# Three heads instead of four biased on GpSimd in tiles 42 to 53 of a log-sum-exp kernel, and constant matmuls from tile 54 on

## The chip, the cores and the metric

The kernel runs on one core of a Trainium2 chip. A core has five engines that run side by side, each with its own queue of instructions in order: TensorE (PE; its weight loads are shown as PEld), VectorE (DVE), ScalarE (ACT), GpSimd (POOL) and SyncE (SP), which issues the loads and stores here. They work on SBUF; PE writes to PSUM, which VectorE and ScalarE can read. The metric is the device time of one execution in microseconds. Before the change three runs took 325.95, 326.36 and 326.98 us, so the median is 326.36 us.

## The reference

The input x has 8 batches of 2048 rows of 2048 columns in fp32 (134 MB), the columns being 8 heads of 256. A bias of 256 values per head is added, and for each row and head the logarithm of the sum of exponentials is taken. Each result is written twice in a row.

```python
x_heads = x.reshape(B, S, H, Dh).transpose(0, 2, 1, 3)
x_heads = x_heads + bias[None, :, None, :]
x_tiled = np.repeat(x_heads, 2, axis=2)
mx = x_tiled.max(axis=-1, keepdims=True)
lse = mx.squeeze(-1) + np.log(np.exp(x_tiled - mx).sum(axis=-1))
```

The output is 8 x 8 x 4096 in fp32. The kernel does not subtract the maximum; it keeps track of the smallest and largest sum and has a second, safe computation behind a branch at its end (`judge`, `all_again`) that is not taken with this data.

## The kernel before, in words

**Tiles.** The rows are cut into 64 tiles (t = 0 to 63) of 2 x 128 rows: 128 partitions, two rows (k = 0, 1) a partition, 2048 columns each, 2 MB a tile. Eight tiles have room in SBUF (`xbs`, seen as `xts`; the profile calls them xb). Up to tile 41 two tiles are loaded by one 4 MB transfer (L174), from tile 42 on each tile has its own, and from tile 57 on each row of a tile (L186); the last tile comes in pieces of columns (`LAST_COLS`). A load into a buffer waits for the last uses of the tile eight before (`last_uses`), and stands in SP's queue.

**The work on a tile.** For each head exp(x + bias) has to be summed over 256 columns. There are several ways to do it, and a dictionary per stage says how many heads go which way:

- Heads 0 to `pe`-1: PE puts the bias into PSUM by a matmul on ones (`put_bias`), adds x by a matmul with the identity, and ScalarE takes the exponential out of PSUM. For the first `acc` heads ScalarE sums as it goes (L373, L393, each followed by an accumulator read); the others go back to the tile in one exponential over two heads (L380).
- Heads from `g0` on: GpSimd adds the bias in place (`g_add`, L412), then ScalarE takes the exponential in place (L418), and VectorE sums with a reduction (L437).
- Heads between `pe` and `g0`: no bias is added. ScalarE takes the exponential of x, and the result is multiplied by exp(bias) (the factors, in `w_ps`, `one_ps` or `w_sb`).

**Stages.** `BULK` (tiles 0 to 53) has pe=3, acc=1, g0=4: heads 0 to 2 by PE, head 3 by a factor, heads 4 to 7 biased by GpSimd. The exponential of heads 3 to 7 is one ScalarE instruction of 2 x 1280 elements; VectorE then multiplies head 3 of both rows by its factor (L430, 512 elements) and sums heads 1 to 7 of both rows in one reduction (L437, 3584 elements). `MIXED` (54 to 56) has pe=1 and g0=4: heads 1 to 3 of each row are weighed and summed by one fused VectorE instruction a head and row (`weigh`, L453, 256 elements, with its accumulator read), and heads 4 to 7 are reduced by L437 (2048 elements). From tile 57 on GpSimd biases nothing; a row at a time, one to three heads go by PE and the rest by factors, weighed on VectorE or, for the last `fold` heads, multiplied and halved on GpSimd (L469, L477) and closed by a small VectorE reduction (L483).

**Order.** The order of instructions on each queue is the order of the program (`manual_schedule`). In the loop's round for tile t come: PE's additions of x; for tiles that aren't bulk, PE's bias of the next unit; GpSimd's addition for t; then what was put off from tile t-1 (`flush(for_pool)`, which runs `later` and with it ScalarE's large exponential of t-1, VectorE's work on it, and SP's reload); and then ScalarE's exponentials of the PE heads of t. From tile 57 on the PE heads of a row are taken by ScalarE only after the exponential of the next row. In round 54 PE also spreads the factors of heads 1 and 2 into `one_ps` (`first_factors`, L235), and ScalarE takes their exponential (L268).

**Constant matmuls.** `keep_warm` (L351 to L355) issues three matmuls of the identity with itself, whose result nobody reads, into the PSUM tile `tp`. It is called once for each row of tiles 57 to 63, after the bias of the next unit. An fp32 matmul is two instructions in the trace, so there are 84.

**The end.** When all sums of the last batch are there, PE transposes them (L606), ScalarE takes the logarithm (L612), SP stores them (L613), and VectorE and PE work out the verdict (L525 to L550).

Of the kernel before, what the change touches and what calls it, by code (L numbers as in the profile page):

```python
# [13 lines left out]
ALU = mybir.AluOpType  # L14
# [7 lines left out]
NBUF = 8  # L22

NEARLY = 5

NWARM = 3

# [1 line left out]

BULK = dict(pe=3, acc=1, g0=4, late=True, fold=0)
MIXED = dict(pe=1, acc=1, g0=4, late=False, fold=0)
PROMPT_F1 = dict(pe=2, acc=2, g0=8, late=False, fold=1)
PROMPT_F2 = dict(pe=2, acc=2, g0=8, late=False, fold=2)
# [9 lines left out]

STAGES = [
    (0, (BULK,)),
    (54, (MIXED,)),  # L50
    (57, (PROMPT_F1, PROMPT_F1)),
    (62, (SINGLE_F1, SINGLE_F1)),
# [10 lines left out]
def kernel(  # L63
# [6 lines left out]
    nc = tc.nc  # L70
    P = nc.NUM_PARTITIONS
    B, S, D = x.shape
    H, Dh = bias.shape
# [2 lines left out]
    NB = S // (P * KB)  # L76
    TB = KB // K
    T = B * NBLK
    T_PROMPT = STAGES[1][0]
    T_FACTORS = T // 2  # L80
    CPE = BULK["pe"] * Dh
    MM = 512
# [67 lines left out]
    def on_x(t, ins, after):  # L150
        buf = users[t // TB % len(xbs)]
        for t_u, u in buf:
            same = u.ins.engine == ins.ins.engine
            if u not in after and (not same or t_u % NBUF == t % NBUF and t_u < t):
                tc.declare_no_dep(
                    ins.ins,
                    u.ins,
                    reason="another tile, or waited for by those it waits for",
                )
        buf.append((t, ins))  # L160
        return ins
# [187 lines left out]
        return heads  # L349

    def keep_warm():  # L351
        for _ in range(NWARM):
            nc.tensor.matmul(  # L353
                tp[:, 0], lhsT=ident, rhs=ident, start=True, stop=True
            )  # L355

    def late_heads(m, t, got, sums):


        mms = []  # L360
        for h, p in enumerate(got[:-1]):
            mm = nc.tensor.matmul(  # L362
                p,
                lhsT=ident,
                rhs=xts[t % NBUF][:, :, h * Dh : (h + 1) * Dh],
                start=False,
                stop=True,
            )
            mms.append(on_x(t, mm, [loads[t, 0, 0]]))

        def pe_part():
            for k in range(K):
                act = nc.scalar.activation(  # L373
                    out=xts[t % NBUF][:, k, 0:Dh],
                    in_=got[0][:, k * Dh : (k + 1) * Dh],
                    func=ACT.Exp,
                    accum_out=sums[:, k, 0:1],
                )
                last_uses[t].append(on_x(t, act, [mms[0]]))
            act = nc.scalar.activation(  # L380
                out=xts[t % NBUF][:, :, Dh : m["pe"] * Dh].rearrange(
                    "p k (h j) -> p h k j", j=Dh
                ),
                in_=got[-1].rearrange("p (h k j) -> p h k j", k=K, j=Dh),
                func=ACT.Exp,
            )
            on_x(t, act, [mms[-1]])

        return pe_part

# [26 lines left out]
    def exp_inplace(t, v, after):  # L417
        return on_x(t, nc.scalar.activation(out=v, in_=v, func=ACT.Exp), [after])  # L418

    def later(m, t, k0, k1, sums, add):  # L420

        h0 = m["pe"] if m["late"] else m["g0"]
        v = xts[t % NBUF][:, k0:k1, h0 * Dh : D]
        done = exp_inplace(t, v, add)
        if m["late"]:
            n = (m["g0"] - h0) * Dh
            f = v[:, :, 0:n]
            h0 = m["acc"]
            v = xts[t % NBUF][:, k0:k1, h0 * Dh : D]
            mul = nc.vector.tensor_tensor(  # L430
                out=f,
                in0=f,
                in1=each_row(w_ps, m["pe"] * Dh - W0, n, k1 - k0),
                op=ALU.mult,
            )
            done = on_x(t, mul, [done])
        red = nc.vector.tensor_reduce(  # L437
            out=sums[:, k0:k1, h0:H],
            in_=v.rearrange("p k (h j) -> p k h j", j=Dh),
            op=ALU.add,  # L440
            axis=mybir.AxisListType.X,
        )
        last_uses[t].append(on_x(t, red, [done]))

    def weigh(t, v, h, dst, after):
        c = h * Dh
# [198 lines left out]
    for t in range(T):  # L645
        if t == T_FACTORS:
            other_factors()
        xt = xts[t % NBUF]
        sums = sums_of(t)
        for k0, k1, c0, c1 in pieces(t):  # L650
            m = modes_of(t)[k0]
            add = None
            heads = []
            if c0 == 0:
                bias_here = bias_there
            if m["late"]:
                pe_part = late_heads(m, t, bias_here, sums)
            else:
                heads = add_x(m, t, k0, c0, c1, bias_here)

                def pe_part(t=t, heads=heads, sums=sums):
                    for k, h, bank, p, mm in heads:
                        sum_biased(t, k, h, bank, p, mm, sums)

            if c0 == 0:
                if next_units and not m["late"]:
                    bias_there = put_bias(*next_units.pop(0))
                if t > T_PROMPT and m["g0"] == H:
                    keep_warm()
                if m["g0"] < H:  # L670
                    add = g_add(m, t, k0, k1)
                if t < T - 1 or k0 == 0:
                    flush(for_pool)
            if t == T_PROMPT and (k0, c0) == (0, 0):
                first_factors()
            h0 = max(c0 // Dh, m["pe"])
            h1 = min(c1 // Dh, m["g0"])
            hf = max(h0, min(h1, H - m["fold"]))
            if h0 < h1 and not m["late"]:
                done = exp_inplace(  # L680
                    t, xt[:, k0:k1, h0 * Dh : h1 * Dh], loads[t, k0, c0]
                )
                if hf < h1:
                    for_pool.append(fold(t, k0, hf, h1, sums, done))
            if c0 == 0:
                flush(for_pe)
            if not m["late"]:
                for k in range(k0, k1):
                    for h in range(h0, hf):
                        weigh(  # L690
                            t,
                            xt[:, k, h * Dh : (h + 1) * Dh],
                            h,
                            sums[:, k, h : h + 1],
                            done,
                        )

            def pool_part(t=t, m=m, k0=k0, k1=k1, sums=sums, add=add):
                if add:
                    later(m, t, k0, k1, sums, add)  # L700
                if k1 == K:
                    reload(t)

            for_pool.append(pool_part)
            if m["g0"] < H:
                pe_part()
                if m["late"]:
                    bias_there = put_bias(*next_units.pop(0))
            elif heads:
                for_pe.append(pe_part)  # L710

        fb, at = divmod(t - 2, NBLK)
        if fb >= 0 and at == NBLK - 1:
            finish(fb)
            ends_of(fb)
            if fb == B - 2:
                store()
# [39 lines left out]
```

## Time and profile before

| | |
|---|---|
| median of three runs | 326.36 us |
| profiled execution | 327.41 us |
| its span, first to last instruction | 325.5 us |
| PE busy | 272.7 us |
| VectorE busy | 289.4 us |
| ScalarE busy | 265.6 us |
| GpSimd busy | 287.5 us |
| read from HBM | 134.23 MB |
| granted PE clock, mean | 0.909 |

A profile page shows one execution. Busy times are per engine. The rows of digits cut the span into 40 slices of about 8.1 us; a digit is the busy share in tenths (9 is 90% or more), or for PEclk the share of PE's full clock that was granted. In a timeline the columns are start, duration, engine, line, operation, tiles written and read, shapes, and how many instructions were merged; in brackets stands how long the engine was idle before and who ended it. SPq is SP's queue. The chain of waits follows the work back from the last instruction, at each step to whatever released it. In a table of windows the columns are the window, its length, the busy time (and number of instructions) of PE, PEld, DVE, ACT and POOL, the granted clock, the busy share of the DMA engines and GB/s.

### The profile page before, as it was taken

The numbers are of one execution on the slowest core, as the hardware profiler recorded it, in microseconds if no ns is written. First come the engines' busy times: TensorE is split into PE (matmuls) and PEld (weight loads), VectorE is DVE, ScalarE is ACT, GpSimd is POOL, SyncE is SP. The second block draws the span as 40 slices with busy tenths as digits, with TensorE's granted clock in tenths as the row PEclk, the third lists the DMA queues.
The fourth block names the chain that finished last, engine by engine and source line by source line (L and its number), as shares of the span: only waits on it lengthen the run. The fifth ranks groups of instructions, "written<-read, shape, count | busy, mean of one in ns | idle before, by whom it ended". The sixth has DMA issues, their size and how long they took to land.

```text
span 325.5 us, 2458 instructions
## 1 busy us (share of the span) xinstructions
PE 272.7 (84%) x695; PEld 102.8 (32%) x695; DVE 289.4 (89%) x329; ACT 265.6 (82%) x426; POOL 287.5 (88%) x120
## 2 busy tenths in 40 slices
PE   5999999878898869888688878698999786598983
PEld 2333333322233323332233323233333232135451
DVE  1346879999999998989989999969999999999996
ACT  1157789898598987889889979869899699989993
POOL 6939997999999899999999999999999999858872
PEclk9977899999597997979899979778999799589999
DMA  8999999999999999999999999999999999999992
GB/s 307 464 403 439 451 417 420 447 439 407 443 443 408 437 435 431 423 439 432 419 443 434 415 443 431 407 433 427 427 421 430 429 424 424 417 421 415 421 391 93
DMA packets 8832, 135.44 MB, mean 416 GB/s; under 512 B 1041, under 2 KB 1425, under 8 KB 2417
## 3 DMA queue, kind: packets, MB, share of 16 engines
q1 hardware_dynamic: 8720, 135.27, 98.0%
q8 instruction: 5, 0.08, 0.1%
q14 instruction: 9, 0.07, 0.1%
q10 hardware_dynamic: 98, 0.01, 0.0%
HBM read 134.23 MB, written 1.05 MB: 416 GB/s over the span
## 4 chain that ended last, share of the span: by engine, by line
DVE 43%; DMA 26%; PE 18%; ACT 8%; POOL 3%; issue 0%; SPq 0%; DVEq 0%
DVE R L437 28%; DMA xb<-in_x_dram 26%; DVE xb L453 9%; PE pair L362 7%; ACT xb L418 6%; DVE xb L430 4%; PE one_ps L362 4%; POOL xb L412 3%; PE pair L303 3%; PE one_ps L303 2%; PE pair L235 1%; ACT xb L380 1%; ACT xb L373 1%; DMA brow<-in_bias_dram 1%; ACT res L507 1%
## 5 line engine op out<-in xcount | busy, mean ns | idle before, releaser
L412 POOL TENSOR_TENSOR xb<-xb,b_rep 128x2048 f32<-128x2048 f32 x57 | 257.3, 4537 | 21.3 <-DMA xb<-in_x_dram 21.1
L437 DVE TENSOR_REDUCE R<-xb 128x14 f32<-128x3584 f32 (+1 forms) x57 | 216.8, 3804 | 1.9
L418 ACT ACTIVATE xb<-xb 128x2560 f32<-128x2560 f32 (+5 forms) x77 | 157.5, 2055 | 8.2 <-POOL xb L412 8.0
L362 PE MATMUL pair<-xb,ident 128*128 128x512 f32 x216 | 117.3, 671 | 0.0
L362 PE MATMUL one_ps<-xb,ident 128*128 128x512 f32 x108 | 68.1, 716 | 10.9 <-DMA xb<-in_x_dram 10.9
L380 ACT ACTIVATE xb<-pair 128x1024 f32<-128x1024 f32 x54 | 56.0, 1038 | 25.0 <-PE pair L362 25.0
L362 PEld LDWEIGHTS pair<-xb,ident 128*128 128x128 f32 x216 | 47.0, 218 | 62.6 <-issue 62.6
L430 DVE TENSOR_TENSOR xb<-xb,w_ps 128x512 f32<-128x512 f32 x54 | 36.8, 681 | 24.0 <-ACT xb L418 23.9
L373 ACT ACTIVATE xb<-one_ps 128x256 f32<-128x256 f32 x108 | 40.4, 387 | 6.7 <-PE one_ps L362 6.7
L303 PEld LDWEIGHTS <-ones 3*128 3x128 bf16 (+1 forms) x192 | 16.8, 95 | 78.0 <-issue 69.0
L303 PE MATMUL one_ps<-b,ones 3*128 3x512 bf16 x49 | 19.1, 390 | 20.9 <-ACT xb L373 20.9
L303 PE MATMUL pair<-b,ones 3*128 3x512 bf16 x98 | 29.1, 376 | 0.0
L362 PEld LDWEIGHTS one_ps<-xb,ident 128*128 128x128 f32 x108 | 17.2, 201 | 33.7 <-DMA xb<-in_x_dram 17.3
L338 PE MATMUL pair<-xb,ident 128*128 128x512 f32 (+1 forms) x36 | 20.5, 656 | 6.3 <-DMA xb<-in_x_dram 6.3
L373 ACT ACTIVATION_READ_ACCUMULATOR xb<-one_ps 128x1 f32 x108 | 23.0, 213 | 0.0
L453 DVE CUSTOM_DVE_ANT_0 xb<-xb,w_ps 128x256 f32<-128x256 f32 x61 | 22.3, 416 | 0.0
L477 POOL TENSOR_TENSOR xb<-xb 128x128 f32<-128x128 f32 (+3 forms) x39 | 13.9, 357 | 3.1
L469 POOL TENSOR_TENSOR xb<-xb,w_sb 128x256 f32<-128x256 f32 (+1 forms) x13 | 10.0, 772 | 5.2 <-ACT xb L418 4.6
L353 PE MATMUL tp<-ident 128*128 128x128 f32 x84 | 13.0, 291 | 0.9 <-ACT res L507 0.9
L507 ACT ACTIVATE res<-tp 32x1024 f32<-32x1024 f32 x7 | 7.1, 1011 | 6.2 <-PE tp L497 6.2
L393 ACT ACTIVATE xb<-pair 128x256 f32<-128x256 f32 x33 | 12.0, 368 | 0.0
L353 PEld LDWEIGHTS tp<-ident 128*128 128x128 f32 x84 | 10.5, 191 | 4.3 <-issue 2.8
(55 smaller groups left out, 91.8 us busy)
## 6 DMA issues: line engine op xcount, KB each, us to landing
xb<-in_x_dram SPq DMA_DIRECT2D x20, 4096.0 KB, 21.3
xb<-in_x_dram SPq DMA_DIRECT2D x17, 2048.0 KB, 22.0
xb<-in_x_dram SPq DMA_DIRECT2D x12, 1024.0 KB, 21.3
xb<-in_x_dram SPq DMA_DIRECT2D x4, 256.0 KB, 13.3
out_dram<-res SPq DMA_DIRECT2D x1, 896.0 KB, 6.8
xb<-in_x_dram SPq DMA_DIRECT2D x2, 384.0 KB, 15.9
xb<-in_x_dram SPq DMA_DIRECT2D x2, 128.0 KB, 6.4
out_dram<-res_last SPq DMA_DIRECT2D x1, 128.0 KB, 1.7
```

Of the source, the lines that this page charges most:

```text
L303: nc.tensor.matmul(p, lhsT=lhsT, rhs=each_row(b, h * Dh, Dh, K), start=i == 0, stop=False,)
L338: mm = nc.tensor.matmul(p, lhsT=ident, rhs=xts[t % NBUF][:, ka:kb, c : c + w], start=False, stop=True,)
L353: nc.tensor.matmul(tp[:, 0], lhsT=ident, rhs=ident, start=True, stop=True)
L362: mm = nc.tensor.matmul(p, lhsT=ident, rhs=xts[t % NBUF][:, :, h * Dh : (h + 1) * Dh], start=False, stop=True,)
L373: act = nc.scalar.activation(out=xts[t % NBUF][:, k, 0:Dh], in_=got[0][:, k * Dh : (k + 1) * Dh], func=ACT.Exp, accum_out=sums[:, k, 0:1],)
L380: act = nc.scalar.activation(out=xts[t % NBUF][:, :, Dh : m["pe"] * Dh].rearrange("p k (h j) -> p h k j", j=Dh), in_=got[-1].rearrange("p ...
L412: add = nc.gpsimd.tensor_tensor(out=v, in0=v, in1=each_row(b_rep, c - G0, D - c, k1 - k0), op=ALU.add)
L418: return on_x(t, nc.scalar.activation(out=v, in_=v, func=ACT.Exp), [after])
L430: mul = nc.vector.tensor_tensor(out=f, in0=f, in1=each_row(w_ps, m["pe"] * Dh - W0, n, k1 - k0), op=ALU.mult,)
L437: red = nc.vector.tensor_reduce(out=sums[:, k0:k1, h0:H], in_=v.rearrange("p k (h j) -> p k h j", j=Dh), op=ALU.add, axis=mybir.AxisListTy ...
L453: ttr = nc.vector.tensor_tensor_reduce(out=v, in0=v, in1=w, scale=1.0, scalar=0.0, op0=ALU.mult, op1=ALU.add, accum_out=dst,)
L477: done = nc.gpsimd.tensor_tensor(out=v[:, :, 0:n], in0=v[:, :, 0:n], in1=v[:, :, n : 2 * n], op=ALU.add)
```

## The change

A new stage, `CATCH`, takes tiles 42 to 53. It differs from `BULK` in g0=5 and fused=True: GpSimd biases heads 5 to 7 (2 x 768 elements) instead of 4 to 7 (2 x 1024). Heads 3 and 4 get no bias; ScalarE's exponential over heads 3 to 7 stays as it is. VectorE then has three steps in place of two: a reduction over heads 1 and 2 of both rows (1024 elements), which waits for the exponential of the PE heads (`pe_done`); four fused instructions, one for each row of heads 3 and 4, that multiply by the factor and sum; and a reduction over heads 5 to 7 (1536 elements). The reduction has moved into a function of its own, `add_up`. Tiles 0 to 41 keep the multiply and the one reduction.

`keep_warm` now issues one matmul of the identity with 384 columns of the spread bias instead of three with 128 columns of the identity. It is called once a row in tiles 54 to 63: twice in each of the tiles 54, 55 and 56 (before, not at all), after the bias of the next unit and, in round 54, before the spreading of the first factors.

```diff
-NWARM = 3
+WARM = 384
-BULK = dict(pe=3, acc=1, g0=4, late=True, fold=0)
+BULK = dict(pe=3, acc=1, g0=4, late=True, fused=False, fold=0)
+CATCH = dict(pe=3, acc=1, g0=5, late=True, fused=True, fold=0)
 STAGES = [
     (0, (BULK,)),
+    (42, (CATCH,)),
     (54, (MIXED,)),
...
-    T_PROMPT = STAGES[1][0]
+    T_PROMPT = STAGES[2][0]
...
     def keep_warm():
-        for _ in range(NWARM):
-            nc.tensor.matmul(
-                tp[:, 0], lhsT=ident, rhs=ident, start=True, stop=True
-            )
+        nc.tensor.matmul(
+            tp.rearrange("p k q -> p (k q)")[:, 0:WARM],
+            lhsT=ident,
+            rhs=b_rep[:, 0:WARM],
+            start=True,
+            stop=True,
+        )
...
-            on_x(t, act, [mms[-1]])
+            pe_done.append(on_x(t, act, [mms[-1]]))
...
+    def add_up(t, k0, k1, h0, h1, sums, after):
+        red = nc.vector.tensor_reduce(
+            out=sums[:, k0:k1, h0:h1],
+            in_=xts[t % NBUF][:, k0:k1, h0 * Dh : h1 * Dh].rearrange(
+                "p k (h j) -> p k h j", j=Dh
+            ),
+            op=ALU.add,
+            axis=mybir.AxisListType.X,
+        )
+        last_uses[t].append(on_x(t, red, [after]))
+
+    def later(m, t, k0, k1, sums, add, pe_done):
+        xt = xts[t % NBUF]
         h0 = m["pe"] if m["late"] else m["g0"]
...
+        done = exp_inplace(t, xt[:, k0:k1, h0 * Dh : D], add)
+        if not m["late"]:
+            add_up(t, k0, k1, m["g0"], H, sums, done)
+        elif m["fused"]:
+            add_up(t, k0, k1, m["acc"], m["pe"], sums, pe_done[0])
+            for k in range(k0, k1):
+                for h in range(h0, m["g0"]):
+                    v = xt[:, k, h * Dh : (h + 1) * Dh]
+                    weigh(t, v, h, sums[:, k, h : h + 1], done)
+            add_up(t, k0, k1, m["g0"], H, sums, done)
+        else:
             n = (m["g0"] - h0) * Dh
...
+            add_up(t, k0, k1, m["acc"], H, sums, on_x(t, mul, [done]))
...
-                if t > T_PROMPT and m["g0"] == H:
-                    keep_warm()
+                if t >= T_PROMPT:
+                    for _ in range(k1 - k0):
+                        keep_warm()
```

## The prediction

> **What bounds the kernel now.** I read the page first, then the chain of waits over the last 44 us, then the timeline of each engine around tile 54 and in the tail.
>
> ```profile
> span 325.5 us, 2458 instructions
> PE 272.7 (84%) x695; PEld 102.8 (32%) x695; DVE 289.4 (89%) x329; ACT 265.6 (82%) x426; POOL 287.5 (88%) x120
> PEclk9977899999597997979899979778999799589999
> DMA  8999999999999999999999999999999999999992
> ```
>
> Four engines are over 80% busy, but the DMA row is full from the second slice to the last but one: loads are never short of work, so only what happens after the last bytes land can become shorter. The last load of x is here:
>
> ```profile
> 312.84 0.33 SPq L186 DMA_DIRECT2D xb<-in_x_dram  x1
> ...
> DMA to landing us min/median/max: 5.3/5.3/5.3
> ```
>
> It is issued at 312.84 and lands 5.3 us later, at 318.15. The span ends at 325.5, so the tail is 7.3 us. What fills it:
>
> ```profile
> by line: DVE xb L453 67.3%; DVE R L437 23.8%; DVE R L483 3.0%; DVE R L453 1.6%; PE w_ps L549 0.9%; DVE ends L525 0.7%; DVE verdict L550 0.6%; DVE ends L528 0.5%; DVE R L525 0.5%; DVE R L528 0.4%; DVE far L541 0.4%; issue 0.4%; DVEq L525 0.0
> ```
>
> From 282 us on the chain is nearly all VectorE (DVE): it works off a backlog without an idle moment. The tail shows how large the backlog still is:
>
> ```profile
> 312.85 1.70 ACT L418 ACTIVATE xb<-xb 128x1792 f32<-128x1792 f32 x1
> ...
> 315.98 0.41 DVE L453 CUSTOM_DVE_ANT_0 xb<-xb,one_ps 128x256 f32<-128x256 f32 x1
> ...
> 319.41 0.41 ACT L393 ACTIVATE xb<-pair 128x256 f32<-128x256 f32 x1
> ...
> 321.19 0.22 DVE L483 TENSOR_REDUCE R<-xb 128x2 f32<-128x64 f32 x1
> ...
> 321.56 0.30 PE L606 MATMUL tp<-ident,R 128*128 128x128 f32 x1 [2.69 <-DVE R L483]
> ```
>
> The second row of tile 62 leaves ScalarE's exponential at 314.55; VectorE takes it up at 315.98, 1.43 us later. ScalarE (ACT) is through with all x at about 319.9 (its last accumulator read ends there), VectorE at 321.4, and the closing transpose (L606) waits for VectorE. ScalarE itself has caught up with the loads: its exponential at 312.85 starts just behind a landing (292.90 + 19.9 us).
>
> **The change, part by part.**
>
> *VectorE in tiles 42 to 53.* Durations, start to start, from the last bulk tiles and the first mixed one:
>
> ```profile
> 269.17 0.68 DVE L430 TENSOR_TENSOR xb<-xb,w_ps 128x512 f32<-128x512 f32 x1
> 269.88 3.89 DVE L437 TENSOR_REDUCE R<-xb 128x14 f32<-128x3584 f32 x1
> 273.68 0.68 DVE L430 TENSOR_TENSOR xb<-xb,w_ps 128x512 f32<-128x512 f32 x1
> ...
> 283.05 0.42 DVE L453 CUSTOM_DVE_ANT_0 xb<-xb,one_ps 128x256 f32<-128x256 f32 x1
> ...
> 283.40 0.42 DVE L453 CUSTOM_DVE_ANT_0 xb<-xb,w_ps 128x256 f32<-128x256 f32 x1
> ...
> 284.76 2.28 DVE L437 TENSOR_REDUCE R<-xb 128x8 f32<-128x2048 f32 x1
> ...
> 286.96 0.41 DVE L453 CUSTOM_DVE_ANT_0 xb<-xb,one_ps 128x256 f32<-128x256 f32 x1
> ```
>
> Removed per tile: one multiply (0.71) and one 3584-wide reduction (3.80), 4.51 us. The reduction of 2048 takes 2.20, so an element costs (3.80 - 2.20)/1536 = 1.042 ns and an instruction 0.07 us. Added: a reduction over heads 1 and 2 (1024 elements, 1.13 us), four fused weighings (0.345 each with their accumulator reads, 1.38), a reduction over heads 5 to 7 (1536 elements, 1.67): 4.18 us. Saved: 0.33 us a tile, 4.0 us over twelve. The ends: if the weighings don't overlap (0.42 each) 0.03 a tile remains, 0.4 us in all; at best 4.1 us. I take 0.33, since weighings run at 0.345 in the mixed tiles beside the same GpSimd addition.
>
> Here a rule speaks against the change. The Trainium skill, VectorE: DVE Perf Modes, section "Rules for kernel authors", advises not to fuse for speed but to keep the number of operations low, and its section on the TRN2 errata fits an fp32 tensor_tensor as (N + 151) cycles at 0.96 GHz. If all these operations had that fixed cost, the two old ones would take 4.58 us and the six new ones 4.68, a loss of 1.2 us over twelve tiles (an estimate from that page). The rows above have a fixed part of about 0.07 us, not 0.16, and they decide.
>
> The first reduction waits only for the exponential of PE's heads, which ScalarE issues ahead of the tile's large exponential; so the added wait holds up nothing behind it in VectorE's queue.
>
> *GpSimd (POOL) in these tiles.* One addition takes 4.54 us at 2048 elements; its 512-wide multiply takes 1.28, so an element costs 2.12 ns, and 1536 take 3.45. That is 1.09 us a tile less. None lies on the path at the end: POOL already starts tile 53 at 268.14, after idling 0.36 us for the landing, and ScalarE's exponential of tile 53 could only move from 272.74 to the end of the PE heads' part before it.
>
> *ScalarE* has the same instructions. *SP* issues the same loads; those of tiles 50 to 61 are released by VectorE up to 4 us earlier, but they queue some 20 us behind other loads, so they land when they do now. Later SP waits for landings anyway. Cost 0, covered by that queue; if it ran dry, an earlier release could only help.
>
> *Matmuls on constants.* In the 14 rows of tiles 57 to 63, six passes of 128 columns (0.94 us) become two of 384. A pass of 512 takes 0.43 at full clock (L362: four in 1.88), so one of 384 takes 0.32 and a row about 0.8 with the pipeline's fill. It lies beside ScalarE, which uses a row's matmuls only after the next row's exponential. Without that cover it would gain 0.1 a row; I count 0.
>
> New are two such matmuls (four passes, 1.29 us) in each of tiles 54, 55 and 56. In tiles 55 and 56 PE idles 2.4 to 2.6 us for the next landing and takes them in. In tile 54 they stand in front of the matmul that spreads the first factors (L235), and ScalarE waits for that:
>
> ```profile
> 274.36 1.02 PE L235 MATMUL one_ps<-brow,ones 1*128 1x512 f32 x2
> ...
> 275.48 0.58 ACT L268 ACTIVATE one_ps<-one_ps 128x512 f32<-128x512 f32 x1 [0.40 <-PE one_ps L235]
> ...
> 282.51 3.29 ACT L418 ACTIVATE xb<-xb 128x2048 f32<-128x2048 f32 x2 [0.44 <-POOL xb L412]
> ...
> 287.50 1.91 ACT L418 ACTIVATE xb<-xb 128x2048 f32<-128x2048 f32 x1 [0.98 <-POOL xb L412]
> ```
>
> L268 moves to 276.77. Behind it in ScalarE's queue stand the exponentials and PE heads of tiles 54 to 56, back to back. But ScalarE idles 0.44 and 0.98 us for POOL there, 1.42 in all, so it stands ready again 0.1 to 0.3 us before POOL is done at 287.47. Net 0, with that little to spare.
>
> *Sum, against the profiled execution.* VectorE starts the weighings of tile 54 when the delayed exponential is done, at about 278.8 instead of 282.72; it waits for ScalarE at tiles 54 and 56 and reaches tile 57 at 292.0 instead of 295.44. From there it needs 1.80 us a row and ScalarE 2.09, so what is left of the lag (1.2 us) is gone by tile 59. In the tail: row two of tile 62 at 314.65 to 316.7, its fold (POOL ends 316.63) to 316.8, four weighings of tile 63's first row to 318.2, five of its second to 319.9 (its last exponential ends 318.8), the last fold to 320.1. ScalarE ends at 319.9 as now. The transpose starts at 320.2 instead of 321.56, and all behind it follows: -1.35 us. The span becomes 324.1 and this execution, 327.41 by its own time (1.9 us outside the span), 326.05. The median of the runs shown, 326.36, lies 1.05 below the profiled execution. If their backlog is the same, the median becomes 325.0. If the 1.05 us are a smaller backlog, only 0.3 is left. I take 325.1, near the first.
>
> **The rivals.**
>
> *The wait moves to ScalarE: slower.* In place of VectorE, ScalarE ends late, because the clock is halved when tile 54 comes. The profile has this state close by:
>
> ```profile
> 276.50:286.50 10.00, 6.21 (x8) 1.70 (x8) 9.96 (x16) 9.56 (x17) 9.17 (x3) 0.50 1.01 418
> ```
>
> There the mixed tiles' matmuls take 2.08 instead of 1.12. With PE waiting for landings in tiles 51 to 53, this can begin earlier. At half clock throughout, the tile's own matmuls (+1.0), the new ones (2.6) and the spread (+1.0) put L268 4.6 to 4.8 us late; 1.5 of that is absorbed up to 287.50, and 3.2 stay, as ScalarE has no idle time from there to 312.8. It would end at 323.0 and the kernel 1.6 us later than now: 328.0. The deciding point is L268 3.0 us late; a half clock of a single 3.4 us stretch gives about 2.9 and no change. Against it: the clock was 1.00 from 260 to 276 in this run, and added matmuls load PE.
>
> The Trainium skill, TensorE: Matmul & The Clock Gate, section "Why this matters for your kernels", asks for gaps between bursts of no more than about 3 us. Here the clock stayed at 0.50 over gaps of 2.56 and 2.36 us. By the rule the state should not occur in these tiles and the sum would be the first one; by the row it can.
>
> *A smaller gain: the landings and ScalarE bound already.* If in usual executions VectorE is only 0.3 to 0.9 us behind ScalarE at the end, that is all to be had: 325.5 to 326.1. For it: the 1.05 us between profile and median, and that ScalarE's end is only 1.5 us ahead of VectorE's. Against: VectorE gains only 0.39 us a tile on the landings (4.51 against 4.9), so each earlier stall leaves a backlog.
>
> *The work saved is none.* If a weighing costs its full 0.42, 0.4 us of backlog goes: 326.0.
>
> **How the numbers follow.** Of a measurement of this kernel about 0.3%, 1 us, can be told from no change. The backlog gone: 0.55, 324.3 to 325.4 (the whole 1.45 us between the two engines' ends and 0.6 of scatter below, the runs shown being 0.4 to 0.6 about their median). Smaller gain or none: 0.25, 325.4 to 327.3. Slower: 0.2, up to 328.0. The range leaves out the outer half of the last: 324.3 to 327.4.
>
> **What would show it.** Right: additions of POOL near 3.45 us and VectorE sets near 4.2 in tiles 42 to 53; VectorE idle, waiting for ScalarE, between 278 and 318; L268 near 276.8; ScalarE's large exponential of tile 56 still at 287.5; L606 waiting for both engines at about 320.2; the last landing near 318.15. Wrong: weighings at 0.42, L268 later than 278.5, ScalarE without idle time before tile 57, or a last landing that moves.

## The result and the profile after

Over 20 runs of each on one chip the changed kernel took 327.20 us (median; 326.67 to 328.7), the kernel before 326.02 us (325.69 to 327.0). The ratio is 1.0035, with a 95% interval of 1.0026 to 1.0045: the change makes the kernel slower, by 1.2 us. The forecast was 325.1 us, so the sign is wrong; the time lies inside the range of 324.3 to 327.4.

The profiled execution of the changed kernel took 327.23 us, so it is a usual one. The head of its page:

```profile
span 325.4 us, 2466 instructions
PE 275.9 (85%) x651; PEld 100.8 (31%) x651; DVE 286.4 (88%) x425; ACT 265.3 (82%) x426; POOL 274.7 (84%) x120
PEclk9977799989959799799778989989999897997998
DMA  7999999999999999999999999999999999999994
```

The work has moved as the edit says. VectorE is busy 3.0 us less, GpSimd (POOL) 12.8 us less. The groups of the new stage (out<-in, shapes, count, busy, mean ns, idle time before):

```profile
L426 DVE TENSOR_REDUCE R<-xb 128x4 f32<-128x1024 f32 x12 | 14.5, 1212 | 0.5 <-ACT xb L385 0.5
...
L426 DVE TENSOR_REDUCE R<-xb 128x6 f32<-128x1536 f32 x12 | 21.0, 1749 | 0.0
...
L417 POOL TENSOR_TENSOR xb<-xb,b_rep 128x1536 f32<-128x1536 f32 x12 | 41.3, 3450 | 12.6 <-DMA xb<-in_x_dram 12.6
```

GpSimd's addition takes 3.45 us, as forecast, and now idles 12.6 us for landings. VectorE's work on one of these tiles:

```profile
255.66 1.21 DVE L426 TENSOR_REDUCE R<-xb 128x4 f32<-128x1024 f32 x1
256.79 0.41 DVE L468 CUSTOM_DVE_ANT_0 xb<-xb,w_ps 128x256 f32<-128x256 f32 x1
...
257.12 0.41 DVE L468 CUSTOM_DVE_ANT_0 xb<-xb,w_ps 128x256 f32<-128x256 f32 x1
...
258.15 2.88 DVE L426 TENSOR_REDUCE R<-xb 128x6 f32<-128x1536 f32 x2
```

The fused weighings start 0.33 to 0.34 us apart, and the next tile's first reduction begins at 259.81: 4.15 us a tile instead of 4.51. So the saving on VectorE is real. It did not reach the end. The chain of waits from 250 us on, by line:

```profile
by line: DMA xb<-in_x_dram 61.0%; ACT xb L423 18.0%; DVE xb L468 6.7%; PE pair L367 3.4%; ACT xb L398 2.9%; PE one_ps L367 2.6%; PE tp L354 2.0%; PE one_ps L237 1.4%; PE pair L340 1.4%; ACT xb L385 1.4%; PE pair L322 0.9%; ACT one_ps L270 0
```

VectorE's backlog is gone: its weighings, 67% of the chain from 282 us on in the execution of before that the forecast was made from, are 11.6% here from the same moment on. In its place stand the landings, and then ScalarE. The last load and the tail, in the timeline:

```profile
314.17 0.33 SPq L188 DMA_DIRECT2D xb<-in_x_dram  x1
314.17 1.70 ACT L423 ACTIVATE xb<-xb 128x1792 f32<-128x1792 f32 x1
...
315.90 0.42 DVE L468 CUSTOM_DVE_ANT_0 xb<-xb,one_ps 128x256 f32<-128x256 f32 x1 [0.26 <-ACT xb L423]
...
320.73 0.41 ACT L398 ACTIVATE xb<-pair 128x256 f32<-128x256 f32 x1
...
321.15 0.22 DVE L498 TENSOR_REDUCE R<-xb 128x2 f32<-128x64 f32 x1
...
321.51 0.30 PE L621 MATMUL tp<-ident,R 128*128 128x128 f32 x1 [1.40 <-DVE R L498]
```

VectorE takes up the second row of tile 62 after waiting 0.26 us for ScalarE: no backlog. But the last load is issued at 314.17 instead of 312.84 and, 5.3 us later as before, lands at 319.48 instead of 318.15. Everything behind it comes 1.3 us later than forecast, the transpose at 321.51 instead of 320.2. The two parts of the change each have a place where this can come from, and both are visible. The first is in the view of the DMA queues, here from 300 to 316 us (queues with packets, MB and share; loads with KB each and us to landing):

```profile
q8 instruction: 1, 0.02, 0.4%
q14 instruction: 1, 0.01, 0.1%
...
xb<-in_x_dram SPq DMA_DIRECT2D x1, 384.0 KB, 16.1
```

Two packets of instructions pass there, one on queue q8 and one on q14, and the load of 384 KB is out 16.1 us. The profile of before has no such packet in this stretch, and there that load is out 15.2 us. The second is tile 54, in ScalarE's timeline:

```profile
278.49 0.58 ACT L270 ACTIVATE one_ps<-one_ps 128x512 f32<-128x512 f32 x1 [2.21 <-PE one_ps L237]
...
288.83 1.94 ACT L423 ACTIVATE xb<-xb 128x2048 f32<-128x2048 f32 x1
```

ScalarE waits 2.21 us for the spread of the first factors. Its exponential of tile 56, at 287.50 before, starts at 288.83, and from there ScalarE has no idle moment up to 314.08, where it stands 1.3 us late too. It then waits 0.10 us for a landing at 314.15. In this execution the two delays lie one on the other; the experiments take them apart.

### The profile page after: what moved, and what is told of

It reads as the page before. It is cut to its first block, busy times and chain, and to the rows that moved or that the text cites. A ratio compares the mean times of both kernels' runs of the same rounds, so it can differ in the third digit from the quotient of the medians.

```text
span 325.4 us, 2466 instructions
## 1 busy us (share of the span) xinstructions
PE 275.9 (85%) x651; PEld 100.8 (31%) x651; DVE 286.4 (88%) x425; ACT 265.3 (82%) x426; POOL 274.7 (84%) x120
## 3 DMA queue, kind: packets, MB, share of 16 engines
HBM read 134.23 MB, written 1.05 MB: 416 GB/s over the span
## 4 chain that ended last, share of the span: by engine, by line
DVE 30%; DMA 28%; PE 25%; ACT 16%; issue 0%; SPq 0%; DVEq 0%; ACTq 0%
DMA xb<-in_x_dram 27%; DVE R L426 23%; PE pair L367 11%; ACT xb L423 10%; PE one_ps L367 6%; DVE xb L468 3%; DVE xb L452 3%; PE pair L305 3%; ACT xb L385 3%; PE one_ps L305 2%; ACT xb L378 1%; PE pair L237 1%; ACT xb L398 1%; ACT res L522 1%; DMA brow<-in_bias_dram 1%
## 5 line engine op out<-in xcount | busy, mean ns | idle before, releaser
L417 POOL TENSOR_TENSOR xb<-xb,b_rep 128x2048 f32<-128x2048 f32 (+1 forms) x57 | 244.6, 4308 | 34.5 <-DMA xb<-in_x_dram 34.5
L426 DVE TENSOR_REDUCE R<-xb 128x14 f32<-128x3584 f32 (+2 forms) x69 | 204.9, 2981 | 2.4 <-ACT xb L385 0.5
L367 PE MATMUL pair<-xb,ident 128*128 128x512 f32 x216 | 119.2, 681 | 0.0
L367 PEld LDWEIGHTS pair<-xb,ident 128*128 128x128 f32 x216 | 47.8, 222 | 64.1 <-issue 64.1
L452 DVE TENSOR_TENSOR xb<-xb,w_ps 128x512 f32<-128x512 f32 x42 | 28.6, 681 | 22.6 <-ACT xb L423 22.6
L468 DVE CUSTOM_DVE_ANT_0 xb<-xb,w_ps 128x256 f32<-128x256 f32 x109 | 39.5, 414 | 2.0 <-ACT xb L423 2.0
L340 PE MATMUL pair<-xb,ident 128*128 128x512 f32 (+1 forms) x36 | 18.6, 600 | 2.8 <-DMA xb<-in_x_dram 2.8
L354 PE MATMUL tp<-b_rep,ident 128*128 128x384 f32 x40 | 17.9, 542 | 3.0 <-ACT res L522 3.0
L468 DVE CUSTOM_DVE_ANT_0 xb<-xb,one_ps 128x256 f32<-128x256 f32 x27 | 10.6, 413 | 1.4 <-ACT xb L423 1.3
L468 DVE DVE_READ_ACCUMULATOR2_ANT R<- 128x1 f32 x137 | 11.1, 81 | 0.0
```

The costliest lines, as they stand in the source:

```text
L340: mm = nc.tensor.matmul(p, lhsT=ident, rhs=xts[t % NBUF][:, ka:kb, c : c + w], start=False, stop=True,)
L354: nc.tensor.matmul(tp.rearrange("p k q -> p (k q)")[:, 0:WARM], lhsT=ident, rhs=b_rep[:, 0:WARM], start=True, stop=True,)
L367: mm = nc.tensor.matmul(p, lhsT=ident, rhs=xts[t % NBUF][:, :, h * Dh : (h + 1) * Dh], start=False, stop=True,)
L417: add = nc.gpsimd.tensor_tensor(out=v, in0=v, in1=each_row(b_rep, c - G0, D - c, k1 - k0), op=ALU.add)
L426: red = nc.vector.tensor_reduce(out=sums[:, k0:k1, h0:h1], in_=xts[t % NBUF][:, k0:k1, h0 * Dh : h1 * Dh].rearrange("p k (h j) -> p k h j" ...
L452: mul = nc.vector.tensor_tensor(out=f, in0=f, in1=each_row(w_ps, h0 * Dh - W0, n, k1 - k0), op=ALU.mult,)
```

## The experiments

Times are medians (range, number of runs); each ratio has its 95% interval, and is taken over all runs, so it can differ from the ratio of the two medians. The nine runs stand in the order e1 to e9. Runs e1 to e4 share one chip and its 35 runs of before (326.05, 325.71 to 327.64). Runs e5 to e8 share another (30 runs of before, 326.07, 325.81 to 327.25), and e9 stands alone (17 runs, 326.13, 325.86 to 327.64).

**The new stage alone**, with the constant matmuls as before (`keep_warm` in its old form, three matmuls of 128 columns, called once a row from tile 57 on):

```diff
-                if t >= T_PROMPT:
-                    for _ in range(k1 - k0):
-                        keep_warm()
+                if t > T_PROMPT and m["g0"] == H:
+                    keep_warm()
```

> The new stage of tiles 42 to 53 alone; the constant matmuls are as before. Theory A (the matmuls in round 54 delay ScalarE, and the usual execution of the kernel before has hardly any VectorE backlog to lose): ratio 0.997 to 1.000, the first factors' exponential starts near 275 to 276, the last load lands near 318.2. Theory B (the new stage itself costs time, by later landings or by its extra instructions): ratio 1.003 to 1.005, the last load lands near 319.5 as in the profile after.

Measured: 326.86 us (326.72 to 327.08, 12), 1.0022 [1.0013, 1.0031]. The stage alone costs 0.8 us, two thirds of the loss, and all twelve runs lie above the median of before. Its ScalarE is not late at tile 54:

```profile
275.43 0.58 ACT L270 ACTIVATE one_ps<-one_ps 128x512 f32<-128x512 f32 x1 [0.81 <-PE one_ps L237]
...
287.51 3.29 ACT L420 ACTIVATE xb<-xb 128x2048 f32<-128x2048 f32 x2 [0.98 <-POOL xb L414]
```

Yet the last load is issued at 313.82 and lands at 319.12. The end of the chain of waits, as the view has it:

```profile
287.51 4.66 ACT xb L420 x3
...
292.91 20.89 DMA xb<-in_x_dram
...
313.82 1.71 ACT xb L420
```

The load issued at 292.91 is out 20.89 us. In the profile of before the one issued at 292.90 was out 19.9 us:

```profile
DMA to landing us min/median/max: 19.9/19.9/19.9
```

The view puts ScalarE ahead of this load, but that is a coincidence in time. SP's own waits from 280 to 320 us name an earlier landing for each of the 13 loads (us in total, times, longest):

```profile
SPq L188 <- DMA xb<-in_x_dram: 31.0, 13, 4.6
```

So a load is issued as soon as an earlier one has landed, here at 303.83 after a landing at 303.77, and ScalarE does not hold it up. The stage makes loads late, without any of the engines that compute being late.

**The constant matmuls alone**, without the new stage: `keep_warm` in its new form, one matmul of 384 columns, in the rows of tiles 54 to 63:

```diff
-                if t > T_PROMPT and m["g0"] == H:
-                    keep_warm()
+                if t >= T_PROMPT:
+                    for _ in range(k1 - k0):
+                        keep_warm()
```

> The constant matmuls alone, as in the changed kernel (one of 384 columns a row, from tile 54); tiles 42 to 53 are as before. Theory A: ratio 1.003 to 1.005, ScalarE's large exponential of tile 56 starts about 1 us later than 287.5. Theory B: ratio 0.999 to 1.001.

Measured: 327.12 us (325.78 to 327.86, 12), 1.0015 [0.9998, 1.0033], in two groups: five runs at 325.78 to 326.03, seven at 327.08 to 327.86. The profile is one of the quick five; in it L268 starts at 276.79 (the forecast said 276.77), the exponential of tile 56 at 287.19, and the last load lands at 317.99. So these matmuls cost nothing in some executions. Whether they make the slower group is not shown by this run: the kernel before has one too, 8 of its 35 runs on this chip at 327.01 to 327.64, and no slower execution was profiled here.

**The changed kernel without the two in round 54:**

```diff
-                if t >= T_PROMPT:
+                if t > T_PROMPT:
```

> The changed kernel without the two constant matmuls in round 54; those of tiles 55 and 56 and of the rows from tile 57 stay. Theory A: the loss goes, ratio to the kernel before 0.997 to 1.000, and the exponential of tile 56 starts at 287.8. Theory B: still 1.003 or more. If only the form of the matmuls from tile 57 on cost something, also 1.003.

Measured: 326.89 us (326.65 to 327.23, 12), 1.0021 [1.001, 1.0032]. That is the time of the stage alone, and the runs above 327.3, eight of the twenty of the changed kernel, are gone. L270 starts at 275.35, the exponential of tile 56 at 287.44, and the last load lands at 319.05, still late. So the constant matmuls of tiles 55 to 63 cost nothing that can be told, those of round 54 about 0.3 us in the median (327.20 - 326.89), and the late landing is not theirs. The intervals of the two ratios overlap, so the size rests on the medians and on the runs above 327.3; the mechanism is shown by the doubling and by the other place below.

**The kernel before, again**, with nothing edited, to see a usual execution: the profile that the forecast was made from took 327.41 us, 1.4 above the median of the 20 runs.

> The kernel before, profiled once more, to see whether the first profile was a usual execution. Its own time, 327.41 us, lay 1.4 us above the median of twenty runs, 326.02. Theory A: a span near 324.2, with VectorE less than 0.5 us behind ScalarE in the second row of tile 62, and ratio 1.000. If the backlog of 1.43 us is there again at a span near 324.2, something else sets the usual time.

Measured: 325.94 us (325.76 to 326.5, 12), 0.999 [0.9977, 1.0003]. Its profiled execution took 325.96 us, with a span of 324.2. The tail of its timeline:

```profile
312.92 0.33 SPq L186 DMA_DIRECT2D xb<-in_x_dram  x1
312.92 1.70 ACT L418 ACTIVATE xb<-xb 128x1792 f32<-128x1792 f32 x1
...
314.65 0.42 DVE L453 CUSTOM_DVE_ANT_0 xb<-xb,one_ps 128x256 f32<-128x256 f32 x1 [0.27 <-ACT xb L418]
...
319.89 0.22 DVE L483 TENSOR_REDUCE R<-xb 128x2 f32<-128x64 f32 x1
...
320.26 0.30 PE L606 MATMUL tp<-ident,R 128*128 128x128 f32 x1 [1.32 <-DVE R L483]
```

This is the tail that the prediction worked out for the changed kernel: second row at 314.65, transpose near 320.2, span 324.1. The kernel before has it already. In the usual execution VectorE waits for ScalarE at tile 62, and there is no backlog to take away; it is an extra of the slower execution that was profiled first. Of the 35 runs of before on this chip 8 lie at 327.01 to 327.64, of the 30 on the next 5 lie above 327; whether all of these carry a backlog is not shown.

*Where the loads lose a microsecond.* The trace has 16 completions for each load of a row, spread over about 2 us, and the load has landed with the last of them. It agrees with the Trainium skill, DMA: Bandwidth & Descriptors, section "Queues, rings and completion order", by which one transfer is split over up to 16 DMA engines. Completions of two loads of the stage alone, in us relative to each one's landing (sorted, worked out from the trace's semaphore updates):

```
landed 300.32:  -2.11 -2.11 -2.00 -1.99 -1.99 -1.92 -1.83 -1.77 -1.46 -1.35 -0.51 -0.49 -0.25 -0.14 -0.01 0.00
landed 303.77:  -3.07 -3.05 -2.95 -2.94 -2.87 -2.80 -2.73 -2.40 -2.27 -1.46 -1.43 -1.41 -1.21 -1.09 -0.95 0.00
```

In the second, fourteen shares have kept their pace against each other. One has fallen back by 1.5 us, from 1.99 ahead of the last to about 0.47 ahead of where the last would have been; a packet of 16 KB on q8, at 299.12, stands ahead of that, and it delays no landing. And one share is 0.95 us behind all the rest. From there on all loads stay late. Between the two landings, at 301.09, a packet of 8 KB passes on the instruction queue q14. In the view of the DMA queues from 300 to 316 us the kernel before, run again, has only x and the results' store (q1), and loads that land on time:

```profile
q1 hardware_dynamic: 1613, 6.54, 101.5%
issues: line engine op xcount, KB each, median us to landing
...
xb<-in_x_dram SPq DMA_DIRECT2D x1, 384.0 KB, 15.2
```

A packet of q8 alone need not make a load late. The run with the wait at tile 54 doubled (below) has it in the same stretch, without one of q14, and its load is out 15.1 us:

```profile
q8 instruction: 1, 0.02, 0.4%
...
xb<-in_x_dram SPq DMA_DIRECT2D x1, 384.0 KB, 15.1
```

Most packets of q14 come at about the same times in all the kernels. Three within the span move with VectorE. The first passes when VectorE has started 48 to 51 instructions (83 in the run with memsets below), the second after 171 to 184, and the third, wherever it comes ahead of the last landing, after 317 to 321. I take them for the refills of VectorE's instructions. That a refill goes through one of the 16 engines that carry x, and that those have no room, is read from the completions: one share is late ever after. The kernel before has 340 instructions of VectorE in its trace, and its third packet comes at 319.67 us, in the second profile at 319.32, behind the last landing. The changed kernel has 436: the four weighings, their accumulator reads and the second reduction, less the multiply, are 8 more instructions a tile, 96 over twelve tiles. Its third packet comes at 302.37, and the second row of tile 60 lands 3.46 us after the row ahead of it instead of 2.50.

**The count alone.** If the number of instructions is what matters, then instructions whose result nobody reads, in the kernel before, at its start, must cost the same:

```diff
+    pad = sb.tile([P, 1], F32, name="pad")
+    for _ in range(96):
+        nc.vector.memset(pad, 1.0)
+
     def first_factors():
```

> The kernel before with 96 one-column memsets on VectorE in its idle time before the first tile (10.6 to 20.2 us); nothing else is changed, nothing left out. Theory F: every 8 KB refill of VectorE's instructions holds up one DMA engine for about 1 us, always the same, and the third one falls before the last landing as soon as VectorE has some 96 more instructions. Then a landing near 300 to 303 us slips by 0.95, the last load lands near 319.1 instead of 318.2, ratio 1.002 to 1.003. Theory B (the new stage's own work or its earlier releases make the landings late): last landing 318.2, ratio 1.000.

Measured: 327.01 us (326.83 to 327.8, 12), 1.0027 [1.0016, 1.0039]. The memsets run from 10.87 to about 22.8 us, 0.12 us each, so VectorE's work on the first tile begins at 22.74 instead of 20.17 us. That has no effect on the loads up to the third packet: a row lands at 300.44, in the kernel before, run again, at 300.39. The third packet comes at 302.08, 280 us behind the memsets, the row after it lands 3.39 us after its predecessor, and the last load at 319.20. The view of its DMA queues from 300 to 316 us, and the end of its chain of waits:

```profile
q14 instruction: 1, 0.01, 0.1%
...
xb<-in_x_dram SPq DMA_DIRECT2D x1, 384.0 KB, 16.1
```

```profile
293.02 20.86 DMA xb<-in_x_dram
...
313.90 1.71 ACT xb L422
```

The same 20.9 and 16.1 us, the same packet, nearly the same time as the stage alone (0.94 us above before instead of 0.81), with none of the stage. This is the cause of the larger part of the loss.

**The wait at tile 54 doubled**: the constant matmuls alone, with four calls in round 54 instead of two.

```diff
-                    for _ in range(k1 - k0):
+                    for _ in range((k1 - k0) * (2 if t == T_PROMPT else 1)):
```

> As the run with the constant matmuls alone, with four of them in round 54 instead of two. Theory A (they delay ScalarE from tile 54 on): the first factors' exponential 1.3 us later than there, ScalarE's exponential of tile 56 at 288.3 or later, all executions about 1.2 us above the fast ones there, ratio 1.004 to 1.006. If the matmuls are covered: same spread of times as there, ratio 1.0015.

Measured: 328.52 us (326.96 to 329.77, 7), 1.0066 [1.0043, 1.009]. That is 1.4 us above the constant matmuls alone (on another chip, where the kernel before takes the same time). The profiled execution is the slowest one:

```profile
275.47 4.54 PE L352 MATMUL tp<-b_rep,ident 128*128 128x384 f32 x8
...
281.16 0.58 ACT L268 ACTIVATE one_ps<-one_ps 128x512 f32<-128x512 f32 x1 [5.19 <-PE one_ps L235]
...
287.63 3.30 ACT L421 ACTIVATE xb<-xb 128x2048 f32<-128x2048 f32 x2
```

Eight passes took 4.54 us, 0.57 each, where 0.32 were counted for a pass at full clock; the granted clock was 0.50 from 277 to 279 us. ScalarE waits 5.19 us, and its exponential of tile 56 follows only at 291.52. The last load lands at 318.19, in time: here the whole loss is ScalarE's, with no late load. So what stands ahead of the spread in round 54 is on the path as soon as it exceeds ScalarE's 1.42 us of slack. L268 came 3 us later than forecast for this run, since the clock was halved under the matmuls.

**The stage for half of the tiles**, 48 to 53, with the constant matmuls as before; 48 more VectorE instructions instead of 96.

```diff
-    (42, (CATCH,)),
+    (48, (CATCH,)),
```

> The new stage alone, for tiles 48 to 53 only: 48 more instructions of VectorE instead of 96. Theory F: the third refill comes about 9 us later, near 310, still before the last landing; slip and loss stay whole, last landing near 319.1, ratio 1.002. Theory B (a price per tile): about half, ratio 1.001, last landing near 318.7.

Measured: 327.55 us (327.13 to 331.12, 12), 1.0079 [1.0046, 1.0111]. The third packet comes later, at 309.71 us, again after 318 instructions, and the slip moves with it, to the row that lands at 311.21 (3.52 us after its predecessor). The cost stays: last landing 319.01, and the quickest run takes 327.13. The packet costs about the same at 309.71 as near 302. Five of the twelve runs took 329.8 to 331.1, which none of this explains; no profile of one was taken, and that stays open.

**The stage with fewer instructions elsewhere.** The fused weighings of tiles 54 to 61 are replaced by plain reductions, so the factors of their heads are left out of the sums; the exponentials and the stage are as in the first experiment. VectorE then has 313 instructions, fewer than before.

```diff
-            if not m["late"]:
+            if not m["late"] and t < 62:
+                add_up(t, k0, k1, h0, hf, sums, done)
+            elif not m["late"]:
                 for k in range(k0, k1):
                     for h in range(h0, hf):
                         weigh(
```

> The new stage alone for tiles 42 to 53, with the weighings of VectorE in tiles 54 to 61 replaced by one plain reduction a unit: the factors of those heads are left out there, and VectorE has 123 instructions less (27 less than the kernel before). Theory F: no third refill before the last landing, which comes back to 318.2; ratio 0.999 to 1.000, without the executions above 327 that the kernel before has. Theory B: last landing still near 319.1, ratio 1.002.

Measured: 325.96 us (325.83 to 326.74, 12), 0.9989 [0.9976, 1.0002]. In its view of the DMA queues from 300 to 316 us there is no packet of instructions, and the load of 384 KB is out 15.1 us:

```profile
q1 hardware_dynamic: 1601, 6.55, 101.5%
issues: line engine op xcount, KB each, median us to landing
...
xb<-in_x_dram SPq DMA_DIRECT2D x1, 384.0 KB, 15.1
```

The last load is issued at 312.75 and lands at 318.08. With the count back below the third packet the stage's loss is gone. No run lies above 326.74, but that does not show that the slower executions of before are gone: the twelve runs of before again had none above 326.5 either. And the median does not get below that of before by more than the measurement resolves. This is an upper bound of what the stage can bring, since part of VectorE's work was left out.

**Round 54's constant matmuls behind the spread** instead of ahead of it, in the changed kernel:

```diff
-                if t >= T_PROMPT:
+                if t > T_PROMPT:
                     for _ in range(k1 - k0):
                         keep_warm()
...
                 first_factors()
+                for _ in range(k1 - k0):
+                    keep_warm()
```

> The changed kernel with the two constant matmuls of round 54 issued behind the spreading of the first factors instead of ahead of it: the same work for PE, another place. If it is their place that costs (theory A), the first factors' exponential starts near 275.5 to 276.8 and the times are those of the run without them, 326.9 and none above 327.3, ratio 1.002. If their mere presence costs (a busier PE, a changed clock), the times stay as after the change, 327.2 with a tail to 328.7, ratio 1.0035.

Measured: 326.88 us (326.71 to 327.13, 12), 1.0016 [1.0004, 1.0027]. In the timeline:

```profile
276.01 0.58 ACT L270 ACTIVATE one_ps<-one_ps 128x512 f32<-128x512 f32 x1 [1.27 <-PE one_ps L237]
...
287.54 3.28 ACT L423 ACTIVATE xb<-xb 128x2048 f32<-128x2048 f32 x2 [0.98 <-POOL xb L417]
```

All the matmuls are there, ScalarE waits for GpSimd again at tile 56, and the time is that of the stage alone. It is their place in front of the spread that costs, not their presence. The last load lands at 319.14, as the third refill makes it.

**Sum.** 326.02 us, plus 0.81 for the refill (326.86 - 326.05), plus about 0.3 for round 54 (327.20 - 326.88), give about 327.1; measured 327.20. This is bookkeeping more than proof, since the last term is taken from the measured 327.20 itself. In the one profiled execution of the changed kernel the landing (319.48) is 0.36 us later than that of the stage alone (319.12), for a reason that is not round 54 (the second refill, see the end). But ScalarE, free only at 314.08 there against a start at 313.82 in the stage alone, would have cost 0.26 anyway. So that execution can't tell the two causes apart, and the 0.3 us rest on the two runs without these matmuls ahead of the spread (326.89 and 326.88).

## Why the prediction was wrong

*VectorE's saving* was right: 4.15 us a tile against 4.18 forecast. The formula of the Trainium skill's page "VectorE: DVE Perf Modes", section on the TRN2 errata, whose fixed cost would have turned it into a loss, gives 0.42 us for a weighing (an estimate from that page), close to the duration in the rows (0.41 to 0.42). But the rows have the next weighing start after 0.33 to 0.34 us, before the last one has ended, so such durations can't be added up. *GpSimd* was right to the digit, 3.45 us. The matmuls on constants from tile 57 on, at 0, were right (the run without the two in round 54).

*"SP issues the same loads … so they land when they do now … Cost 0"* failed, and with it "the last landing near 318.15". The landing moved to 319.48. That earlier releases change nothing was right: up to 300.32 us the stage alone lands its rows as the kernel before, run again, does (300.39). But the step looked only at when loads are issued and released. What it missed is that VectorE's instructions come over the same 16 DMA engines, and that 96 more of them, four weighings with accumulator reads a tile, bring a third 8 KB refill ahead of the last load. This measured 0.81 us (0.94 with the memsets). The prediction named "a last landing that moves" as a sign against it, but had no mechanism that could move it, and none of its rivals was this one. A second sign against it came too, ScalarE without idle time between L270 and tile 57, but the quick execution of the constant matmuls alone has it as well, at no cost.

The Trainium skill, Runtime: NRT & Kernel Launch, section "Instruction fetch mechanics", says that the sequencer fetches instructions over a DMA queue of its own, in blocks, at a cost that is mostly hidden. The queue of its own agrees with the trace (q14). The cost was hidden from VectorE, which had no idle moment within 4 us of the packet at 302.37. It was not hidden from the loads, which fill the DMA engines and lost 0.95 us for good.

*"If their backlog is the same, the median becomes 325.0 … I take 325.1, near the first"* failed by the choice. The kernel before, run again, has no backlog in a usual execution; the 1.43 us that VectorE lagged belonged to an execution 1.4 us above the median. The prediction saw the sign for it, 1.05 us between profile and median, and the rival *smaller gain* (325.5 to 326.1) fits this part: the stage with fewer instructions took 325.96, though with some of VectorE's work left out. The mechanism, landings and then ScalarE as the bound once VectorE has caught up, is right, and its tail (314.65, 320.2) stands in the run of before line for line.

*Tile 54, "Net 0, with that little to spare"* failed, by its margin. At the changed kernel's tile 54 the PE timeline shows:

```profile
268.45 1.95 PE L367 MATMUL one_ps<-xb,ident 128*128 128x512 f32 x2 [0.55 <-DMA xb<-in_x_dram]
...
274.40 1.12 PE L340 MATMUL pair<-xb,ident 128*128 128x512 f32 x2
275.46 0.39 PE L322 MATMUL pair<-b,ones 3*128 3x512 bf16 x1
275.77 1.56 PE L354 MATMUL tp<-b_rep,ident 128*128 128x384 f32 x4
277.26 1.12 PE L237 MATMUL one_ps<-brow,ones 1*128 1x512 f32 x2
```

The first additions of tile 53 ran at half speed (1.95 us for two passes that take 1.12 at 274.40; the granted clock was 0.55 from 268.4 to 270.4), so ScalarE waited 1.75 us for the PE heads and tile 54's addition could begin only at 274.40, 1.3 us later than in the profile of before. The four passes took 1.56 us where 1.29 were counted. L270 came at 278.49 instead of 276.77, and of the delay 1.3 us went through to tile 56. A like wait for the PE heads (1.81 to 1.93 us) stands in three profiles with nothing ahead of the spread (before again, the memsets, the stage with fewer instructions); there the factors' exponential came at 276.38 to 276.92, within the slack. In these profiles it takes both, the slow start at tile 53 and the matmuls. This is the slower rival's mechanism, the clock halved when tile 54 comes, in a smaller dose: by its own bound (L268 3.0 us late decides) this is 3.0 us late. But the sum put that rival at 328.0 and it explains only 0.3 us in the median. In single executions it costs more: with the two matmuls in front of the spread runs reach 328.7, without them or with them behind it 327.2. In the quick execution of the constant matmuls alone L268 was where the prediction had it, and the cost was 0.

The rival that the clock stays low was decided the other way round: it stood at 0.50 from 276.5 to 286.5 before, and after the change at 1.00, as the windows of the changed kernel show (columns as in the prediction):

```profile
276.50:286.50 10.00, 8.00 (x21) 2.99 (x19) 8.55 (x29) 8.02 (x13) 9.17 (x3) 1.00 1.01 418
```

In the other profiles the same window stands at 0.50 to 0.62 where the mixed tiles have no added matmuls (five executions) and at 0.66 to 0.86 where they have (four). So the clock stood higher there in every execution profiled with the added matmuls; it brought no time, since ScalarE waits for GpSimd or for the landings behind it.

## What to carry to other kernels

Where the DMA engines are full to the end, an instruction has a second price: count the instructions of each engine before and after a change, and see whether one more refill comes ahead of the last load. Here 96 instructions cost as much at the very start, with a result that nobody reads, as when they did the work. And before a backlog in one profiled execution is taken for a gain, set that execution's own time beside the median: the difference, 1.05 us, was most of the forecast gain of 1.26.

## What the runs showed of the hardware

- An 8 KB refill of VectorE's instructions put one of the 16 shares 0.95 to 1.02 us back, for all later loads. The packet itself takes only 0.33 us; why the loss is three times that is open. The trace does not name the DMA engine of a share, but by the order of the completions the third refill hit the share that the second had made the last (the changed kernel, the stage for half of the tiles). Whether a refill shows depends on that share's lead. When it was 0.84 us ahead of the last one, the landing moved by 0.13 us (before again, at 294.59); when it was already the last, by 0.96 (the changed kernel, at 302.37).
- The packets of q8 are of 16 KB and come every 230 to 270 instructions of PE and its weight loads, so I take them for PE's refills. The one at 299.12 in the stage alone took 1.07 us and put one share from 1.99 us ahead of the last to about 0.47 ahead, and no landing moved.
- The changed kernel's second refill, at 253.49 us, also moved a landing by 0.48 us (5.38 us after its predecessor instead of 4.90), which that of the stage alone did not. The share had a lead of 0.50 us there and of 0.99 in the stage alone. Why it was smaller is open.
- A kernel with all of the computation and quicker than both was not made and stays untried. By the run with fewer instructions it would, as an estimate, have to do the stage with some 90 fewer VectorE instructions than the change has, for at most the 0.24% that this run's interval allows.
